# Dilated attention with the tokens of each block of 128 sorted by residue of 16, one stacked query tile and doubled key tiles

## The chip, the cores and the metric

The kernel runs on one core of a Trainium2 chip. The time is device microseconds (us) of one execution on that core; less is better. The engines are called as in the profile: PE (matrix products), PEld (its loading of the stationary operand), DVE (VectorE), ACT (ScalarE), POOL (GpSimd) and SP (it issues all DMAs here).

## What is computed

One decoder layer over 4096 tokens of width 1024, in float32. Eight attention heads of width 64 mix three dilated windows; four heads of width 128 run a gated linear recurrence (HGRN2). Both halves are normalised, gated, joined, projected, added to the input and normalised. The part that the change is about, cut from the reference:

```python
DILATED_PATTERNS = ((128, 1), (512, 4), (2048, 16))      # (window, dilation)

def _dilated_window_attn(q, k, v, window, dilation):
    # the sequence is split into `dilation` residue sub-sequences; on each a causal
    # band of width window//dilation = 128, swept in blocks of 128 queries
    qb, kb, vb = to_blocks(q), to_blocks(k), to_blocks(v)
    kw, vw = with_prev(kb), with_prev(vb)                 # the block before and this one
    scores = jnp.einsum('bhrnqe,bhrnke->bhrnqk', qb, kw) * (e ** -0.5)
    scores = jnp.where(mask, scores, -jnp.inf)
    m = jnp.max(scores, axis=-1)
    p = jnp.exp(scores - m[..., None])
    l = jnp.sum(p, axis=-1)
    o = jnp.einsum('bhrnqk,bhrnke->bhrnqe', p, vw)
    return from_blocks(o), from_blocks(m), from_blocks(l)
```

For each query the outputs `o` of the three dilations are weighted by `exp(m - max m)` and divided by the weighted sum of the `l`.

## The kernel before

Float32 products are made of two float32r parts, hi + lo. The work has three phases.

Phase 1 (to about 590 us) projects x for the first three pairs of attention heads, block of 128 tokens by block, and writes queries and keys transposed (feature on the partition, token along the row; hi and lo parts), values and gates to DRAM (`attn_rows`, L274).

Phase 2 (to about 2480 us) first projects the fourth pair of heads, then runs the four recurrence heads, two blocks at a time: `project_T` and `project_N` (L226, L240, their matmuls are L220), `hgrn_gates`, `hgrn_values`, `hgrn_block`. x for the next two blocks is loaded and split while this one runs: ACT writes `xhi` (L209), POOL writes `xlo = raw - xhi` (L210). In between, `take` (L614) advances a generator that emits attention work at a fixed rate, so that all eight heads are spread evenly; a scheduler then orders every engine's instructions by its own estimate of time. Each engine runs its list in order.

A head (L483) runs its patterns in the order d = 16, 4, 1. Each pattern has 16 calls of `score` (L413), two blocks of queries each. `score` makes, for each block, two products into one PSUM bank: the queries' 128 columns are the stationary operand, the keys' 128 or 256 columns stream as the moving operand. K1 holds the keys' hi part on partitions 0 to 63 and the lo part on 64 to 127; Q1 holds the queries' hi part twice, Q2 the lo part twice. For a dilation d the columns are taken with stride d from rows in token order:

```python
def cols(t, r, d, j, n, p=slice(None)):
    a = r + d * 128 * j
    return t[p, a : a + d * (128 * n - 1) + 1 : d]
```

So with d = 16 a block of queries is 128 floats that lie 64 bytes apart, with d = 4 they lie 16 bytes apart, with d = 1 side by side. Then DVE adds the mask and takes the row maximum (L434), ACT takes the exponential and the row sum (L436), `flip` (L440) transposes the weights on PE (L446) and splits them on ACT (L449) and DVE (L450), `weigh` (L453) multiplies them with the values, ACT copies one half (`other`, L461) and DVE adds it: for d = 16 and 4 into the tile OA at stride d (L528, L543), for d = 1 into o1 (L551). `exchange` (L467) sends the row maxima and sums of d = 16 and 4 through DRAM to bring them into token order; `arrive` (L477) fetches them into `nat`. After every eight blocks of d = 1, `finish` (L564) joins the patterns: DVE writes the three weighted outputs to `pr` (L589), POOL adds them into `num` (L592, L593), the norm factor `nrr` is worked out on DVE (its last step is L147), POOL multiplies (L600, L601), and SP issues the DMA of `num` to y_d (L602). The next head's queries and keys are loaded during d = 1 (L409 to L411).

Phase 3 is the output projection, the residual and the last norm.

Of the kernel before, what the change touches and what calls it, by code (L numbers as in the profile page):

```python
# [17 lines left out]
F32 = mybir.dt.float32  # L18
F32R = mybir.dt.float32r
# [8 lines left out]
S = 4096  # L28
# [21 lines left out]
def layer(ctx: ExitStack, tc: tile.TileContext, x, xT, xP, pos, w_in, w_out, nw, anw, hnw, lbraw, fnw,  # L50
# [21 lines left out]
    mask = const.tile([128, 256], F32, name="mask")  # L72
# [13 lines left out]
    nrstd = const.tile([128, NB], F32, name="nrstd")  # L86
# [35 lines left out]
    def lower_bounds():  # L122
        """1 - lower bound of the forget gates, to DRAM"""
# [12 lines left out]
    def rsqrt(pool, u, n, scale, eps, tag):  # L136
        """(u*scale + eps) ** -0.5, [128, n], with one Newton step"""
# [62 lines left out]
    def load_pair(t):  # L200
        """two blocks of x, transposed: four pairs of k tiles"""
# [12 lines left out]
    def accumulate(groups):  # L214
        """groups of products, each into its own columns of one bank"""
# [10 lines left out]
    def project_T(X, W):  # L226
        """the first 256 columns of the group, transposed, for two blocks"""
# [12 lines left out]
    def project_N(X, W):  # L240
        """the last 256 columns of the group, two blocks of rows"""
# [21 lines left out]
    def row_stats(b):  # L263
        r = rsqrt(p1p, ssq[:, b : b + 1], 1, 1.0 / D, EPS, "rs")
        V.tensor_copy(rstd[:, b : b + 1], r)
        V.tensor_scalar(nrstd[:, b : b + 1], r, -1.0, None, op0=ALU.mult)

    def sigm(e):
        """e = exp(-z) -> sigmoid(z), in place; the bound keeps Ln in its range"""
# [4 lines left out]
    def attn_rows(pool, p, b, ps, gv, pt_):  # L274
# [3 lines left out]
        # rotary on the first 16 dims of q and k  # L278
# [20 lines left out]
        # silu of the gate times the norm gain  # L299
# [50 lines left out]
    def hgrn_values(t, ps):  # L350
        """gates and values of two blocks, tokens on the partitions"""
# [5 lines left out]
        for n in range(2):  # L357
            b = 2 * t + n
            A.activation(gv[:, n], ps[:, 256 * n : 256 * (n + 1)], AF.Copy, scale=rstd[:, b : b + 1])
# [6 lines left out]
    def hgrn_block(hh, b, qd, kd, g):  # L366
# [46 lines left out]
    def score(h, d, r, j0, ml, loc):  # L413
        """exp(score - row maximum) of two blocks of queries, row maxima and sums"""
# [4 lines left out]
        for j in (j0, j0 + 1):  # L419
# [3 lines left out]
            T.matmul(o, cols(Q1, r, d, j, 1), cols(K1, *ks), start=True, stop=False)  # L423
            T.matmul(o, cols(Q2, r, d, j, 1), cols(K1, *ks), start=False, stop=True)  # L424
            parts.append((j, nk, o, off))
            off += 128 * nk
        for j, nk, o, off in parts:
# [6 lines left out]
            V.tensor_tensor_reduce(out=p_, in0=o, in1=mask[:, 256 - 128 * nk : 256], scale=-0.125, scalar=3e38,  # L434
# [5 lines left out]
    def flip(d, j0, nb, loc):  # L440
        """transpose the weights of two blocks of keys and split them"""
# [11 lines left out]
    def weigh(seq, out):  # L453
        """seq: (values, unit, first column block, blocks)"""
# [391 lines left out]
```

## Time and profile before

| | |
|---|---|
| Time, median of three runs (lowest, highest) | 2859.76 us (2859.27, 2865.69) |
| The profiled execution: span | 2859.0 us |
| Granted TensorE clock | 0.988 of full speed |
| DVE, ACT, POOL busy, share of the span | 67%, 62%, 32% |
| DMA moved | 387.64 MB, mean 136 GB/s |

Busy time of PE is modelled: matmuls are pipelined, and the duration of one is longer than the step from one to the next. What a matmul takes from PE is therefore read from the timeline, as the distance between its start and the start of the next one. In the windows a row gives, after the stretch and its length, the busy time of PE, PEld, DVE, ACT and POOL with the count of instructions in brackets, then the granted clock, the share of the DMA engines and GB/s. In the rows of instructions the last pair of numbers is the total busy time in us and the mean of one in ns.

The heads can be told apart by the 96 weight loads of L423 that each makes, 32 in each pattern. The fifth head's scores begin at 1563 us (d = 16), 1620 us (d = 4) and 1684 us (d = 1), its last score is at 1767 us, and the sixth head begins at 1791 us.

### The profile page before, as it was taken

To read this page: it belongs to the slowest core of one execution; us is meant where nothing else is said; L and a number is where in the kernel's file an instruction comes from. 1 tells how busy PE (TensorE), PEld (TensorE's weight loads), DVE (VectorE), ACT (ScalarE), POOL (GpSimd) and SP (SyncE) were. 2 spreads that over 40 slices of the span, in tenths; PEclk is the share of its full clock that TensorE was granted. 3 is DMA by queue.
4 is the path that set the end of the run, shared out by engine and by line. 5 is a ranking of instruction groups with operands and counts; after the bars stand their busy time and mean duration, and the time that the engine had idled before them with its cause. 6 is when DMAs were issued, how large, how long until landed. Compare 5 with 4: busy or idle time off the path is not lost.

```text
span 2859.0 us, 53619 instructions
## 1 busy us (share of the span) xinstructions
PE 2779.3 (97%) x17697; PEld 2505.0 (88%) x17697; DVE 1907.3 (67%) x5907; ACT 1761.3 (62%) x5174; POOL 913.8 (32%) x906
## 2 busy tenths in 40 slices
PE   7999999999999999999999999999999999999998
PEld 5888888878888999998999999999999999788887
DVE  6444444446787788788688688778878878844443
ACT  6444444447766777776777777777777777622222
POOL 2222222143344245235335335335434524300000
PEclk9999999999999999999999999999999999899999
DMA  6444444494475265255346355336436422643432
GB/s 217 141 140 140 144 140 137 139 247 144 138 211 144 78 161 130 78 152 147 90 124 158 82 150 151 100 93 164 115 97 173 124 78 71 185 147 133 137 136 85
DMA packets 448138, 387.64 MB, mean 136 GB/s; under 512 B 117064, under 2 KB 340724, under 8 KB 447860
## 3 DMA queue, kind: packets, MB, share of 16 engines
q1 hardware_dynamic: 447860, 384.21, 47.1%
q8 instruction: 141, 2.31, 0.4%
q14 instruction: 137, 1.12, 0.1%
HBM read 291.27 MB, written 92.82 MB: 134 GB/s over the span
## 4 chain that ended last, share of the span: by engine, by line
PE 54%; DVE 10%; ACT 3%; DMA 2%; issue 1%; POOL 0%; SPq 0%; ACTq 0%; POOLq 0%; DVEq 0%
PE proj L220 18%; PE att L423 5%; PE po L458 5%; PE att L424 4%; PE proj L196 4%; PE proj L195 4%; PE proj L197 4%; PE att L446 4%; PE hp L370 1%; DVE pt L434 1%; PE hp L742 1%; PE hp L372 1%; DVE pl L450 1%; PE hp L378 1%; PE hp L380 1%
## 5 line engine op out<-in xcount | busy, mean ns | idle before, releaser
L195 PE MATMUL proj<-whi,xhi 128*128 128x512 f32 x1280 | 510.8, 399 | 15.9 <-ACT whi L171 7.9
L197 PE MATMUL proj<-whi,xlo 128*128 128x512 f32 x1280 | 513.2, 401 | 0.0
L196 PE MATMUL proj<-wlo,xhi 128*128 128x512 f32 x1280 | 510.4, 399 | 1.3 <-DVE wlo L172 1.3
L210 POOL TENSOR_TENSOR xlo<-raw,xhi 128x512 fp32r<-128x512 f32 x256 | 336.5, 1319 | 385.1 <-ACT xhi L209 343.7
L434 DVE CUSTOM_DVE_ANT_0 pt<-att,mask 128x256 f32<-128x256 f32 (+1 forms) x768 | 271.7, 390 | 158.6 <-PE att L424 155.5
L220 PE MATMUL proj<-xhi,whi 128*128 128x256 f32 x1024 | 301.3, 294 | 6.4 <-DVE hz L329 2.4
L423 PE MATMUL att<-K,Q 128*128 128x256 f32 (+1 forms) x768 | 302.2, 401 | 2.5 <-DMA Q<-qk_d 1.3
L220 PE MATMUL proj<-xhi,wlo 128*128 128x256 f32 x1024 | 300.9, 294 | 0.9 <-DVE wlo L172 0.9
L195 PEld LDWEIGHTS proj<-whi,xhi 128*128 128x128 f32 x1280 | 242.6, 190 | 67.3 <-ACT whi L171 8.8
L220 PE MATMUL proj<-xlo,whi 128*128 128x256 f32 x1024 | 301.3, 294 | 0.0
L220 PE MATMUL proj<-whi,xhi 128*128 128x256 f32 x1024 | 298.0, 291 | 0.0
L220 PE MATMUL proj<-whi,xlo 128*128 128x256 f32 x1024 | 297.2, 290 | 0.0
L220 PE MATMUL proj<-wlo,xhi 128*128 128x256 f32 x1024 | 296.6, 290 | 0.0
L196 PEld LDWEIGHTS proj<-wlo,xhi 128*128 128x128 f32 x1280 | 242.1, 189 | 53.9 <-DVE wlo L172 3.2
L436 ACT ACTIVATE pt<-pt,ml 128x256 f32<-128x256 f32 (+1 forms) x512 | 238.3, 467 | 77.2 <-DVE ml L434 75.5
L197 PEld LDWEIGHTS proj<-whi,xlo 128*128 128x128 f32 x1280 | 242.3, 189 | 48.0
L424 PE MATMUL att<-K,Q 128*128 128x256 f32 (+1 forms) x768 | 276.6, 367 | 2.1 <-issue 2.1
L450 DVE TENSOR_TENSOR pl<-att,ph 128x512 fp32r<-128x512 f32 (+1 forms) x384 | 238.3, 624 | 45.6 <-ACT ph L449 42.0
L185 POOL TENSOR_TENSOR xlo<-raw,xhi 128x512 fp32r<-128x512 f32 x126 | 162.2, 1289 | 244.9 <-ACT xhi L184 220.6
L282 DVE SCALAR_TENSOR_TENSOR rot<-rt,rsin 128x32 f32<-128x32 f32 x128 | 56.1, 438 | 271.9 <-ACT rt L277 271.7
L449 ACT ACTIVATE ph<-att 128x512 fp32r<-128x512 f32 (+1 forms) x384 | 206.9, 542 | 49.7 <-PE att L446 45.1
L446 PE MATMUL att<-ident,pt 128*128 128x128 f32 x1368 | 223.5, 278 | 6.4 <-DVE nat L434 5.1
(201 smaller groups left out, 7388.5 us busy)
## 6 DMA issues: line engine op xcount, KB each, us to landing
raw<-xP SPq DMA_DIRECT2D x256, 256.0 KB, 3.6
raw<-xT SPq DMA_DIRECT2D x128, 256.0 KB, 2.8
qk_d<-stk SPq DMA_DIRECT2D x128, 256.0 KB, 2.9
vh<-v_d SPq DMA_DIRECT2D x128, 256.0 KB, 3.5
Q<-qk_d SPq DMA_DIRECT2D x224, 128.0 KB, 3.7
raw<-x SPq DMA_DIRECT2D x64, 256.0 KB, 2.6
v_d<-hl SPq DMA_DIRECT2D x128, 128.0 KB, 2.6
vh<-v_d SPq DMA_DIRECT2D x128, 128.0 KB, 2.5
```

Source lines behind the costliest of these rows:

```text
L195: T.matmul(ps, hi[:, c], whi, start=(k == 0), stop=False)
L196: T.matmul(ps, hi[:, c], wlo, start=False, stop=False)
L197: T.matmul(ps, lo[:, c], whi, start=False, stop=(k == KT - 1))
L210: G.tensor_tensor(lo, raw, hi.bitcast(F32), op=ALU.subtract)
L220: m = T.matmul(o, l, r, start=first is None, stop=(k == KT - 1 and g == len(groups) - 1 and n == 2))
L423: T.matmul(o, cols(Q1, r, d, j, 1), cols(K1, *ks), start=True, stop=False)
L424: T.matmul(o, cols(Q2, r, d, j, 1), cols(K1, *ks), start=False, stop=True)
L434: V.tensor_tensor_reduce(out=p_, in0=o, in1=mask[:, 256 - 128 * nk : 256], scale=-0.125, scalar=3e38, op0=ALU.add, op1=ALU.min, accum_out=m)
L436: A.activation(p_, p_, AF.Exp, scale=-1.0, bias=m, accum_out=l)
L446: T.transpose(ps[:, n * 128 : (n + 1) * 128], loc[u], ident)
L449: A.activation(ph[:, :w], ps[:, :w], AF.Copy)
L450: V.tensor_sub(pl[:, :w], ps[:, :w], ph[:, :w].bitcast(F32))
```

## The change

Within every block of 128 tokens the token `16 u + r` is stored in place `8 r + u`. A residue class of 16 is then a run of 8 neighbours in every block, 32 bytes, and a residue class of 4 is four such runs that lie 32 places apart. A band of a dilated pattern is read as runs of 8 floats.

What follows from it, edit by edit:

- The host gives x, its transpose for phase 1 and the positions in that order; the transpose for the recurrence stays in token order. The row norms of the recurrence are turned back (`rstdn`). The recurrence writes y with four DMAs for four blocks, rows in the new order, and `out` is written back in token order.
- The mask has one pair of triangles for each dilation, as the order within a block differs.
- Instead of K1, Q1, Q2 there are KH (hi twice), KL (lo twice) and QS (hi over lo). Both products of a block now have the same stationary queries. For d = 16 and 4 POOL first copies 512 query columns into a contiguous tile `qc` (two buffers), once for two calls of `score`: 16 copies a head, 128 in all. For d = 1 the queries are read in place.
- OA is written in runs of 8. The values are loaded with four DMAs instead of two (d = 16) or one (d = 4).
- `exchange` transposes the maxima and sums on PE, DVE copies them to `mt`, and four (d = 16) or eight (d = 4) DMAs write them, in place of two; `mt` and `mr` share one buffer.
- To make room, `num` lies in `pr` now, and `hrb` has one buffer instead of two.

The diff also empties comments, so that line numbers shift. Its core:

```diff
 def cols(t, r, d, j, n, p=slice(None)):
-    a = r + d * 128 * j
-    return t[p, a : a + d * (128 * n - 1) + 1 : d]
+
+    return t[p].rearrange("p (g r u) -> p r g u", r=d, u=8)[:, r, 16 * j : 16 * (j + n)]
...
-        rb = hp.tile([128, 256], F32, name="hrb", bufs=2)
+        rb = hp.tile([128, 256], F32, name="hrb", bufs=1)
...
-            dma(y_d[b0 * 128 : (b0 + 4) * 128, 512 + hh * 128 : 512 + (hh + 1) * 128].rearrange("(i p) c -> p i c", p=128),
-                gv[:, :, 128:256])
...
+            yv = y_d[b0 * 128 : (b0 + 4) * 128, 512 + hh * 128 : 512 + (hh + 1) * 128].rearrange("(i r u) c -> i u r c", r=16, u=8)
+            for i in range(4):
+                dma(yv[i], gv[:, i, 128:256])
...
-        for t, u0, u1 in ((K1, 1, 3), (Q1, 0, 0), (Q2, 2, 2)):
+        for t, u0, u1 in ((KH, 1, 1), (KL, 3, 3), (QS, 0, 2)):
             dma(t[0:64, cs].bitcast(F32), qk[:, u0, cs])
             dma(t[64:128, cs].bitcast(F32), qk[:, u1, cs])
...
+    def queries(d, r, j0):
+
+        if d == 1:
+            return QS[:, 128 * j0 : 128 * (j0 + 4)]
+        q = tp.tile([128, 512], F32R, name="qc", bufs=2)
+        if d == 16:
+            v = QS.rearrange("p (g r u) -> p r g u", r=16, u=8)[:, r : r + 2]
+            G.tensor_copy(q.rearrange("p (r g u) -> p r g u", r=2, u=8), v)
+        else:
+            G.tensor_copy(q.rearrange("p (g u) -> p g u", u=8), cols(QS, r, d, j0, 4))
+        return q
+
+    def score(h, d, r, j0, q, ml, loc):
...
-            T.matmul(o, cols(Q1, r, d, j, 1), cols(K1, *ks), start=True, stop=False)
-            T.matmul(o, cols(Q2, r, d, j, 1), cols(K1, *ks), start=False, stop=True)
+            T.matmul(o, q[:, j % 2 * 128 : (j % 2 + 1) * 128], cols(KH, *ks), start=True, stop=False)
+            T.matmul(o, q[:, j % 2 * 128 : (j % 2 + 1) * 128], cols(KL, *ks), start=False, stop=True)
...
+        ps = ps_t.tile([64, 128], F32, name="att")
+        T.transpose(ps, ml.rearrange("i q c -> i (q c)"), ident)
+        mt = tp.tile([64, 128], F32, name="mt", tag="mr", bufs=1)
+        V.tensor_copy(mt, ps)
         for q in range(2):
-            dma(md[q].rearrange("(b i r) -> i b r", i=128, r=d), ml[:, q, :].rearrange("i (b r) -> i b r", r=d))
...
+                for r in range(d):
+                    dma(mv[r], mt[32 * q + r : 32 * (q + 1) : d].rearrange("j (g u) -> j g u", u=8))
...
-                            for n2 in range(2):
-                                dma(vh[:, 2 * n2 : 2 * n2 + 2].bitcast(F32), sv[:, r + n2, :, i, :])
+                            for n2 in range(4):
+                                dma(vh[:, n2].bitcast(F32), sv[r + n2 // 2, n2 % 2, :, :, i, :])
...
-                        V.tensor_tensor(cols(OA, r, 4, j0, 4, slice(64, 128)), po[64:128], other(po, 64), op=ALU.add)
+                        V.tensor_tensor(cols(OA, r, 4, j0, 4, slice(64, 128)), po[64:128].rearrange("p (g u) -> p g u", u=8),
+                                        other(po, 64).rearrange("p (g u) -> p g u", u=8), op=ALU.add)
...
-        num = tp.tile([128, 8, 64], F32, name="num", bufs=1)
-        G.tensor_tensor(num, pr[:, :, 0], pr[:, :, 1], op=ALU.add)
+        num = pr[:, :, 1]
+        G.tensor_tensor(num, pr[:, :, 0], num, op=ALU.add)
...
-        "pos": np.ascontiguousarray(positions[0].reshape(NB, 128).T),
+        "pos": np.ascontiguousarray(positions[0].reshape(NB, 8, 16).transpose(2, 1, 0).reshape(128, NB)),
```

How the change moves instructions is seen at two places. The first is POOL's list at the fourth head's last `finish` and the start of the fifth head; numbers behind a name count its buffers. Before:

```order
L592 TENSOR_TENSOR num_19886<-pr_19692 128x512
L593 TENSOR_TENSOR num_19886<-num_19886,pr_19692 128x512
L363 TENSOR_TENSOR hgv_20173<-hgv_20173,heg_20513 128x2x128
L364 TENSOR_TENSOR hgv_20173<-hgv_20173,gv0H_16451 128x2x128
L600 TENSOR_TENSOR num_19886<-num_19886,nrr_19895 128x512
L601 TENSOR_TENSOR num_19886<-num_19886,sgt_19680 128x512
L210 TENSOR_TENSOR xlo_20884<-raw_20881,xhi_20883 128x512
L332 TENSOR_TENSOR hz_20799<-hz_20799,he_20800 128x256
L210 TENSOR_TENSOR xlo_20890<-raw_20887,xhi_20889 128x512
```

The same place after the change, where L622, L629 and L630 are the sums and products of `finish` and L420 is the copy of queries for d = 16:

```order
L622 TENSOR_TENSOR pr_20035<-pr_20035 128x8x64
L331 TENSOR_TENSOR hz_21546<-hz_21546,he_21547 128x256
L210 TENSOR_TENSOR xlo_21641<-raw_21638,xhi_21640 128x512
L420 COPY qc_20593<-QS_6195 128x512
L210 TENSOR_TENSOR xlo_21647<-raw_21644,xhi_21646 128x512
L344 TENSOR_TENSOR hqd_21564<-hz_21546,hea_21561 128x256
L420 COPY qc_20648<-QS_6195 128x512
L210 TENSOR_TENSOR xlo_22002<-raw_21999,xhi_22001 128x512
L362 TENSOR_TENSOR hgv_21250<-hgv_21250,heg_21619 128x2x128
L629 TENSOR_TENSOR pr_20035<-pr_20035,nrr_20237 128x8x64
L363 TENSOR_TENSOR hgv_21250<-hgv_21250,gv0H_16703 128x2x128
L630 TENSOR_TENSOR pr_20035<-pr_20035,sgt_20023 128x8x64
```

The copies stand between the `xlo` tiles of the recurrence's projection and the steps of `finish`, and wait for their turn behind these.

The second place is DVE's list between the norm factor of the fourth head's second `finish` (L147) and the first weighted output of the next `finish`. Before (L589 is that output):

```order
L147 TENSOR_TENSOR nrr<-nrr,nrq 128x8
L450 TENSOR_TENSOR pl<-att,ph 128x512
L329 TENSOR_TENSOR hz<-proj,hrb 128x512
L388 TENSOR_TENSOR hR<-hp_19949,hs 128x128
L270 TENSOR_SCALAR he<-he 128x512
L589 TENSOR_TENSOR pr<-att,wt 128x2x192 x2
```

After the change (L618 is that output):

```order
L147 TENSOR_TENSOR nrr<-nrr,nrq 128x8
L580 TENSOR_TENSOR o_19600<-po,pot 64x256
L462 TENSOR_TENSOR pl<-att,ph 128x512
L580 TENSOR_TENSOR o_19600<-po,pot 64x256
L334 SCALAR_TENSOR_TENSOR hcum<-keep,hcum 128x256
L336 TENSOR_SCALAR hhalf<-hcum 128x2
L339 TENSOR_SCALAR hcum<-hcum,hhalf 128x128 x2
L383 TENSOR_SCALAR hs<-hR,hea 128x128
L618 TENSOR_TENSOR pr<-att,wt 128x2x192 x2
```

The weighted outputs of the next `finish` have moved back by four instructions here. Counted over the three such places of each of the seven later heads, the distance from L147 to the first output is 7 instructions on the average before and 13 after.

More of the change, by code (lines that the diff above doesn't have):

```diff
@@ L433, in score @@
             p_ = pt[:, off : off + 128 * nk]
-            V.tensor_tensor_reduce(out=p_, in0=o, in1=mask[:, 256 - 128 * nk : 256], scale=-0.125, scalar=3e38,
+            V.tensor_tensor_reduce(out=p_, in0=o, in1=mask[:, (1, 4, 16).index(d), 256 - 128 * nk : 256], scale=-0.125, scalar=3e38,
                                    op0=ALU.add, op1=ALU.min, accum_out=m)
@@ L470, in exchange @@
         md = ml_d[h, di]
+        ps = ps_t.tile([64, 128], F32, name="att")
+        T.transpose(ps, ml.rearrange("i q c -> i (q c)"), ident)
+        mt = tp.tile([64, 128], F32, name="mt", tag="mr", bufs=1)
+        V.tensor_copy(mt, ps)
         for q in range(2):
-            dma(md[q].rearrange("(b i r) -> i b r", i=128, r=d), ml[:, q, :].rearrange("i (b r) -> i b r", r=d))
-        mr = tp.tile([32, 2, 128], F32, name="mr", bufs=1)
+            if d == 16:
+                mv = md[q].rearrange("(j g r u) -> j r g u", g=16, r=d, u=8)
+                for j in range(2):
+                    dma(mv[j], mt[32 * q + 16 * j : 32 * q + 16 * (j + 1)].rearrange("r (g u) -> r g u", u=8))
+            else:
+                mv = md[q].rearrange("(j g r u) -> r j g u", g=16, r=d, u=8)
+                for r in range(d):
+                    dma(mv[r], mt[32 * q + r : 32 * (q + 1) : d].rearrange("j (g u) -> j g u", u=8))
+        mr = tp.tile([32, 2, 128], F32, name="mr", tag="mr", bufs=1)
         dma(mr, md.rearrange("q (b i) -> b q i", i=128))
@@ L502, in head @@
                     _, r, j = ready[n]
-                    score(h, d, r, j, ml, loc[r])
+                    if n % 2 == 0:
+                        qc = queries(d, r, j)
+                    score(h, d, r, j, qc[:, 256 * (n % 2) : 256 * (n % 2 + 1)], ml, loc[r])
                     yield 1.0
@@ L511, in head @@
                         if d == 16:
-                            for n2 in range(2):
-                                dma(vh[:, 2 * n2 : 2 * n2 + 2].bitcast(F32), sv[:, r + n2, :, i, :])
+                            for n2 in range(4):
+                                dma(vh[:, n2].bitcast(F32), sv[r + n2 // 2, n2 % 2, :, :, i, :])
+                        elif d == 4:
+                            for n2 in range(4):
+                                dma(vh[:, n2].bitcast(F32), sv[r, j + n2, :, :, i, :])
                         else:
-                            dma(vh.bitcast(F32), sv[:, r, j : j + 4, i, :])
+                            dma(vh.bitcast(F32), v_d[p][j * 128 : (j + 4) * 128, i, :].rearrange("(j p) c -> p j c", p=128))
                         fl = {}
@@ L526, in head @@
                         po = weigh(seq, None)
-                        pv = po.rearrange("p (r u) -> p r u", r=2)
-                        V.tensor_tensor(OA[0:64].rearrange("p (u r) -> p r u", r=16)[:, r0 : r0 + 2, :],
-                                        pv[0:64], other(po, 0).rearrange("p (r u) -> p r u", r=2), op=ALU.add)
+                        pv = po.rearrange("p (r g u) -> p r g u", r=2, u=8)
+                        V.tensor_tensor(OA[0:64].rearrange("p (g r u) -> p r g u", r=16, u=8)[:, r0 : r0 + 2],
+                                        pv[0:64], other(po, 0).rearrange("p (r g u) -> p r g u", r=2, u=8), op=ALU.add)
                         yield 1.0
@@ L786, in final_norm @@
         V.scalar_tensor_tensor(xr, xr, r, fnwt, op0=ALU.mult, op1=ALU.mult)
-        dma(out[b * 128 : (b + 1) * 128, :], xr)
+        dma(out[b * 128 : (b + 1) * 128, :].rearrange("(u r) c -> r u c", r=16), xr)
     for b in range(2):
@@ L819 @@
     i = np.arange(128)
-    t1 = np.where(i[:, None] <= i[None, :], 0.0, NEG).astype(f)
-    t2 = np.where(i[:, None] >= i[None, :], 0.0, NEG).astype(f)
+    ms = []
+    for m in (16, 4, 1):
+        n = m * (i // (8 * m) * 8 + i % 8) + i // 8 % m
+        for lower in (False, True):
+            ms.append(np.where((n[:, None] >= n[None, :]) if lower else (n[:, None] <= n[None, :]), 0.0, NEG).astype(f))
     arrays = {
-        "x": xs,
+        "x": xc,
         "xT": xT,
         "xP": np.ascontiguousarray(xs.reshape(NB // 2, 256, KT, 128).transpose(0, 3, 2, 1)).reshape(NB // 2, 128, 2 * D),
-        "pos": np.ascontiguousarray(positions[0].reshape(NB, 128).T),
+        "pos": np.ascontiguousarray(positions[0].reshape(NB, 8, 16).transpose(2, 1, 0).reshape(128, NB)),
         "w_in": w,
```

31 lines of the change are left out of this document (16 added, 15 removed).

## The prediction

> **What bounds the kernel now.** I read the page's busy times first, then the windows of one head, then the timeline of PE inside them. The page:
>
> ```profile
> PE 2779.3 (97%) x17697; PEld 2505.0 (88%) x17697; DVE 1907.3 (67%) x5907; ACT 1761.3 (62%) x5174; POOL 913.8 (32%) x906
> ```
>
> PE looks full, but its durations overlap, so this alone proves nothing. The windows of the fifth head, in the order d = 16, d = 4, d = 1 and the last `finish` (columns as in the table's text: PE, PEld, DVE, ACT, POOL):
>
> ```profile
> 1563.00:1620.00 57.00, 57.00 (x419) 55.27 (x418) 42.78 (x142) 44.45 (x143) 25.29 (x24) 1.00 0.37 100
> 1620.00:1684.00 64.00, 63.94 (x458) 60.96 (x458) 45.88 (x137) 48.12 (x142) 16.03 (x16) 1.00 0.32 84
> 1684.00:1767.00 83.00, 81.29 (x669) 77.16 (x668) 72.98 (x215) 64.37 (x196) 40.00 (x37) 1.00 0.63 175
> 1767.00:1791.00 24.00, 20.97 (x175) 19.70 (x174) 22.36 (x49) 15.77 (x45) 15.36 (x16) 1.00 0.65 164
> ```
>
> In the first two PE has no idle time, while ACT is busy 78% and 75%. In d = 1 DVE is at 88% and PE idles 1.71 us (2%); in the last `finish` DVE is at 93% and PE idles 3.03 us (13%). So time taken off PE in d = 16 and d = 4 shortens the kernel until ACT or DVE comes near 90%.
>
> **What the strides cost PE.** The timeline of PE, one `score` call with d = 16, then two recurrence matmuls of 128 contiguous columns (first column start, second duration):
>
> ```profile
> 1572.12 0.36 PE L423 MATMUL att<-K,Q 128*128 128x128 f32 x1
> 1572.31 0.39 PE L424 MATMUL att<-K,Q 128*128 128x128 f32 x1
> 1572.52 0.50 PE L423 MATMUL att<-K,Q 128*128 128x256 f32 x1
> 1572.85 0.40 PE L424 MATMUL att<-K,Q 128*128 128x256 f32 x1
> 1573.06 0.30 PE L220 MATMUL proj<-xhi,wlo 128*128 128x256 f32 x1
> ...
> 1574.12 0.39 PE L378 MATMUL hp<-hgv,hk 128*128 128x128 f32 x2
> 1574.35 0.39 PE L380 MATMUL hp<-hgv,att 128*128 128x128 f32 x2
> ```
>
> Two calls with d = 4:
>
> ```profile
> 1641.23 0.58 PE L423 MATMUL att<-K,Q 128*128 128x256 f32 x1
> 1641.62 0.42 PE L424 MATMUL att<-K,Q 128*128 128x256 f32 x1
> 1641.86 0.42 PE L423 MATMUL att<-K,Q 128*128 128x256 f32 x1
> 1642.10 0.41 PE L424 MATMUL att<-K,Q 128*128 128x256 f32 x1
> 1642.34 0.30 PE L220 MATMUL proj<-whi,xlo 128*128 128x256 f32 x1
> ...
> 1642.60 0.49 PE L423 MATMUL att<-K,Q 128*128 128x256 f32 x1
> ...
> 1643.62 0.30 PE L220 MATMUL proj<-wlo,xhi 128*128 128x256 f32 x1
> ```
>
> One call with d = 1, where both operands are contiguous already:
>
> ```profile
> 1515.52 0.28 PE L423 MATMUL att<-K,Q 128*128 128x256 f32 x1
> 1515.64 0.29 PE L424 MATMUL att<-K,Q 128*128 128x256 f32 x1
> 1515.76 0.28 PE L423 MATMUL att<-K,Q 128*128 128x256 f32 x1
> 1515.88 0.28 PE L424 MATMUL att<-K,Q 128*128 128x256 f32 x1
> 1515.99 0.28 PE L220 MATMUL proj<-wlo,xhi 128*128 128x256 f32 x1
> ```
>
> The same four matmuls take 0.47 us with d = 1 and 1.11 and 1.02 us with d = 4, about 1.07. The call with d = 16 has two matmuls of 128 and two of 256 columns and takes 0.94 us; contiguous it would be 2 x 0.115 (L378: 0.23 for two) + 2 x 0.12 = 0.47.
>
> **The change part by part.**
>
> *PE's term.* If queries from `qc` and keys in runs of 8 go at the contiguous rate, d = 16 saves 16 x (0.94 - 0.47) = 7.5 us a head. d = 4 has, for each residue, one call like the one above (0.47 saved) and three of 256 columns throughout (1.07 - 0.48 = 0.59 saved): 4 x 0.47 + 12 x 0.59 = 9.0, together 16.5 a head. Eight heads: 132 us.
>
> Runs of 8 floats as a moving operand occur in no row. The upper end is the contiguous rate. The lower end is that keys stay as slow as now. That rate is seen alone where the weights loaded next are contiguous: from L424 to L220 it is 0.21 us (d = 16) and 0.24 us (d = 4) for 256 columns. Then d = 16 needs 2 x 0.115 + 2 x 0.21 = 0.65 and saves 0.29 x 16 = 4.6; d = 4 needs 0.96 in place of 1.07 (12 x 0.11 = 1.3) and 0.71 in place of 0.94 (4 x 0.23 = 0.9): 6.8 a head, 54 us. I take 132, since d = 4 steps 16 bytes and d = 16 64 bytes and both are slow by about the same factor: the price looks like one for every float that stands alone, not for distance.
>
> [...]
>
> *What becomes the next limit.* d = 16 shrinks from 57 to 49.5 us with ACT's 44.45 us unchanged (90%), d = 4 from 64 to 55 with 48.12 (87%). By the windows above PE then idles between 2% (companion at 88%) and 13% (93%); I take 3% of 104.5 us, 3.1 a head, 25 us in all. Ends: 0 and 13% (13.6 a head, 109 us).
>
> *DVE.* The writes to OA lose their stride:
>
> ```profile
> L543 DVE TENSOR_TENSOR OA<-po,pot 64x512 f32<-64x512 f32 x64 | 71.3, 1114 | 7.7 <-ACT pot L464 5.8
> L528 DVE TENSOR_TENSOR OA<-po,pot 64x512 f32<-64x512 f32 x64 | 66.8, 1044 | 5.8 <-ACT pot L464 5.8
> L450 DVE TENSOR_TENSOR pl<-att,ph 128x512 fp32r<-128x512 f32 x216 | 146.7, 683 | 22.5 <-ACT ph L449 20.3
> ```
>
> At L450's 0.68 they free 64 x 0.43 + 64 x 0.36 = 51 us of DVE (0 if runs of 8 do not help it). Against that stand POOL's 128 copies. Nearest rows: a one-input operation on 256 columns and a two-input one on 512.
>
> ```profile
> L113 POOL TENSOR_SCALAR kk<-kk 128x256 f32<-128x256 f32 x1 | 0.7, 722 | 0.1
> L592 POOL TENSOR_TENSOR num<-pr 128x512 f32<-128x512 f32 x32 | 42.7, 1334 | 44.9 <-DVE pr L589 30.0 <-PE proj L220 7.5 <-issue 6.4
> ```
>
> Between 0.72 and 1.33 I take 0.9, the nearer to the one-input row: 14.4 us a head on POOL's 96.7 (the four windows), so 111 of some 212. POOL is no bound, but DVE feels it. The duration of one DVE instruction on SBUF alone, min/median/max, and its mean:
>
> ```profile
> L340 DVE TENSOR_SCALAR hcum<-hcum,hhalf x128: 251/281/1385, 897.5 to 2457.9; 128x128 f32<-128x128 f32 x128
> ...
> L340 DVE TENSOR_SCALAR hcum<-hcum,hhalf 128x128 f32<-128x128 f32 x128 | 60.9, 512 | 1.4
> ```
>
> The mean is 0.23 us over the median, and the longest lasts about one POOL instruction more. POOL is busy 42% of the head; copies add 7 points, so about 0.04 us for each of some 150 such instructions in a head (counted in the code: about 13 for each two blocks, nine times, and nine in each `finish`): 6 us a head, 48 in all. It cancels the 51; I count 0, between -51 and +48. [...]
>
> *`num` inside `pr`.* The next `finish` may write `pr` only when the DMA of y has read it. The second `finish` of the fourth head, from DVE's and POOL's timelines and the DMA list:
>
> ```profile
> 1533.29 0.17 DVE L147 TENSOR_TENSOR nrr<-nrr,nrq 128x8 f32<-128x8 f32 x1
> 1536.15 1.01 DVE L589 TENSOR_TENSOR pr<-att,wt 128x384 f32<-128x384 f32 x2
> ...
> 1534.66 1.29 POOL L601 TENSOR_TENSOR num<-num,sgt 128x512 f32<-128x512 f32 x1
> ...
> y_d<-num SPq DMA_DIRECT2D x32, 256.0 KB, 3.5
> ```
>
> From L147 to the landing it takes 2.66 + 3.5 = 6.2 us; today L589 follows after 2.9. Behind a waiting L589 stand the score maxima and the recurrence's steps, which PE needs. The new order puts 13 instead of 7 instructions in between; at 0.40 us each (22.36/49 = 0.46 and 72.98/215 = 0.34 in the last two windows) that is 5.2 us, and 1.0 remains. Three such places a head: 24 x 1.0 = 24 us. Ends: 0 and 24 x 3.3 = 79.
>
> *Small terms.* Sixteen more transposes with their copies and the longer chain of `exchange`: PE has waited at `arrive` only this much in all,
>
> ```profile
> PE att L480 <- DVE nat L434: 0.6, 1, 0.6
> ```
>
> so there is slack; I put 0.4 us for each, 6 us. The new DMA issues (40 more a head for values, 8 for `exchange`, 96 for the recurrence's y) come on SP, which now waits long for its own turn:
>
> ```profile
> SPq L515 <- PE po L458: 125.1, 42, 13.1
> ```
>
> They fit into that slack, and cost nothing as long as it stays; without it, an issue delays only loads that are asked for early. `hrb` with one buffer is refilled when the last block pair's first DVE step is done, some 25 us ahead: nothing. Copies at a head's start behind POOL's `finish` steps: one POOL instruction, 0.75 us, eight times: 6 us. Phases 1 and 3 keep their work.
>
> *The sum*, on the span of 2859.0 us: -132 + 25 + 24 + 6 + 6 = -71, 2788. The median of the runs lies 0.8 us above the span: **2789 us**.
>
> **The rivals.**
>
> 1. *Everything hides* (chance 0.10): idle, `pr` and the small terms near 0. For it: PE is never idle now in d = 16 and 4. Against: ACT at 90%. 2859.8 - 132 = 2728, some 2735 with the transposes.
> 2. *The keys do not get faster* (0.10): the change then does half of what it says. 54 us gained, no new idle time as ACT stays at 85%, 36 us of other terms: 2842.
> 3. *ACT takes over* (0.08): 13% idle as in the last `finish`: -132 + 109 + 36 = +13, 2873; halfway it is no change.
> 4. *Copies queue on POOL* (0.10), the way to slower. POOL runs in order, and its `xlo` often wait:
>
> ```profile
> POOL xlo L210 <- ACT xhi L209: 343.7, 134, 16.1
> ```
>
> That is 2.6 us a time. A copy behind such a wait holds PE's two next calls of `score`. If half the 128 copies pass 2.6 us on, the price is 166 us: 2789 - 6 + 166 = 2949. It decides from 71/128 = 0.55 us a copy. Against it: two `qc` buffers give a copy the time of two calls, 57/8 = 7 us.
>
> **How the numbers follow.** The forecast holds 0.62. A measurement here tells 0.3% (8.6 us) from no change. Faster: 0.61 of the forecast, rivals 1 and 2, and 0.03 of rival 3, so 0.84; the same: 0.05; slower: 0.11. The range runs from rival 1 to rival 2, 2733 to 2842, and leaves out rivals 3 and 4.
>
> **What would show it.** The steps of the score matmuls with d = 16 and 4 at 0.12 us for 256 columns; at 0.21 rival 2 holds. The window of d = 16 near 51 us, of d = 4 near 57, with ACT near 88%. DVE waiting before L618 for the DMA of y, about 1 us a time. A copy near 0.9 us; PE waiting for `qc` would mean rival 4. If phases 1 or 3 change by over 3 us, I have missed a part.

## The result and the profile after

The changed kernel takes **2789.25 us** (median of 4 runs, 2788.09 to 2791.51), the kernel before in the same comparison 2859.52 us (4 runs, 2858.64 to 2865.69): ratio 0.9751, 95% interval 0.9737 to 0.9765. That is 70 us faster, and the forecast of 2789 us holds almost to the digit. Its terms hold less well, and that is what the rest is about.

The profiled execution has a span of 2788.2 us. Its page, the line of busy times:

```profile
PE 2672.7 (96%) x17714; PEld 2386.1 (86%) x17714; DVE 1875.9 (67%) x5892; ACT 1745.6 (63%) x5174; POOL 994.0 (36%) x1034
```

PE lost 106.6 us of busy time and the span 70.8: some 36 us came back as idle time. The timeline of PE, one `score` call with d = 16 and one with d = 4, each with the matmul behind it:

```profile
1572.22 0.23 PE L435 MATMUL att<-KH,qc 128*128 128x128 f32 x1
1572.28 0.27 PE L436 MATMUL att<-KL,qc 128*128 128x128 f32 x1
1572.39 0.35 PE L435 MATMUL att<-KH,qc 128*128 128x256 f32 x1
1572.57 0.31 PE L436 MATMUL att<-KL,qc 128*128 128x256 f32 x1
1572.72 0.29 PE L220 MATMUL proj<-xhi,whi 128*128 128x256 f32 x1
...
1635.87 0.28 PE L435 MATMUL att<-KH,qc 128*128 128x256 f32 x1
1635.98 0.28 PE L436 MATMUL att<-KL,qc 128*128 128x256 f32 x1
1636.10 0.28 PE L435 MATMUL att<-KH,qc 128*128 128x256 f32 x1
1636.22 0.28 PE L436 MATMUL att<-KL,qc 128*128 128x256 f32 x1
1636.34 0.28 PE L470 MATMUL po<-ph,vh 128*128 128x256 f32 x1
```

From the first start to the start of the next matmul it is 0.50 us (0.94 before) and 0.47 us (about 1.07 before). The d = 4 call runs at the rate of contiguous keys; d = 16 takes 0.03 us more than foreseen.

The windows of the fifth head, cut at the first score of each stage (PE, PEld, DVE, ACT, POOL, then clock, DMA share and GB/s):

```profile
1556.00:1609.00 53.00, 51.68 (x433) 49.86 (x431) 43.48 (x142) 44.62 (x146) 29.79 (x31) 1.00 0.39 104
1609.00:1662.00 53.00, 49.20 (x400) 46.67 (x400) 43.08 (x136) 46.81 (x140) 17.64 (x20) 1.00 0.44 126
1662.00:1750.00 88.00, 85.06 (x710) 80.47 (x710) 73.97 (x219) 65.21 (x201) 43.12 (x42) 1.00 0.62 157
1750.00:1775.00 25.00, 23.32 (x192) 22.01 (x192) 22.75 (x55) 16.11 (x48) 15.90 (x16) 1.00 0.54 144
```

d = 16 went from 57 to 53 us (foreseen 51) and d = 4 from 64 to 53 (foreseen 57), with ACT at 84% and 88%. PE, which had no idle time there, now idles 1.32 and 3.80 us. But d = 1 grew from 83 to 88 us, and its PE has 710 matmuls in place of 669: work that used to lie beside the slow scores now lies there. A stage by itself is therefore no measure of the gain. Summed over the seven later heads, from the starts of the first score of each stage (in us; a last `finish` is the stretch from one head's last score to the next head's first, and the seven of them begin with the first head's, so the columns do not add up to the last one):

| | d = 16 | d = 4 | d = 1 | last `finish` | second head's first score to the last score |
|---|---|---|---|---|---|
| before | 416 | 447 | 570 | 167 | 1574 |
| after | 375 | 382 | 592 | 183 | 1508 |

The two strided stages gave 106 us, the other two took 38 back. Ahead of the second head and behind the last score only 5 us of the 71 were won.

The whole attention phase in one window, before and then after, in which PE's idle time is the length less its busy time:

```profile
590.00:2481.00 1891.00, 1835.79 (x13403) 1736.43 (x13402) 1481.66 (x4368) 1375.52 (x4128) 767.46 (x725) 0.99 0.49 131
```

```profile
590.00:2410.20 1820.20, 1729.73 (x13426) 1618.64 (x13424) 1450.36 (x4377) 1360.70 (x4127) 847.61 (x853) 0.98 0.51 138
```

PE work fell by 106.1 us, PE idle time rose from 55.2 to 90.5. Everything in the result is these two numbers: -106 + 35 = -71. The phases ahead of it and behind it changed by some 3 us: PE starts its 2,500th matmul at 578 us before and 581 after, and from the 16,000th of the 17,714 to the end it takes 372 us before and 369 after (before counted in the same proportion).

The groups of DVE and POOL that the prediction priced (busy time, mean ns | idle before):

```profile
L571 DVE TENSOR_TENSOR OA<-po,pot 64x512 f32<-64x512 f32 x64 | 44.5, 695 | 6.6 <-ACT pot L476 4.9
L556 DVE TENSOR_TENSOR OA<-po,pot 64x512 f32<-64x512 f32 x64 | 43.3, 677 | 5.7 <-ACT pot L476 5.6
L339 DVE TENSOR_SCALAR hcum<-hcum,hhalf 128x128 f32<-128x128 f32 x128 | 67.1, 562 | 1.4
L420 POOL CAST qc<-QS 128x512 fp32r<-128x512 f32 x64 | 40.7, 643 | 48.0 <-PE att L436 41.8 <-DMA QS<-qk_d 5.6 <-DMA raw<-xP 0.6
L422 POOL CAST qc<-QS 128x512 fp32r<-128x512 f32 x64 | 39.6, 618 | 112.1 <-PE att L436 111.7 <-PE proj L220 0.3
```

The writes to OA take 0.68 and 0.70 us in place of 1.04 and 1.11, as forecast. A copy takes 0.63 us, less than the 0.9 assumed. The copies wait for PE (L436 gives their buffer back), so they run ahead of it; no wait of a matmul names `qc`, and one weight load waited for it, for 0.4 us. The DVE instruction in which the prediction saw the collisions with POOL went from a mean of 512 to 562 ns, +0.05 us (foreseen +0.04); the kernel without copies shows below that the copies are not the reason.

Last, the place at which `pr` is held. In the third `finish` of the fourth head POOL ends the last product (L630) at 1545.5 us. The timeline of SP's queue, which then issues the DMA of y (L631):

```profile
1538.38 0.53 SPq L206 DMA_DIRECT2D raw<-xP  x1
1545.68 0.64 SPq L403 DMA_DIRECT2D y_d<-hgv  x1
...
1550.20 0.54 SPq L631 DMA_DIRECT2D y_d<-pr  x1
```

and the timeline of DVE, where the next `finish` begins with L618:

```profile
1550.38 0.35 DVE L383 TENSOR_SCALAR hs<-hR,hea 128x128 f32<-128x128 f32 x1
1554.90 1.49 DVE L618 TENSOR_TENSOR pr<-att,wt 128x384 f32<-128x384 f32 x3 [4.18 <-DMA y_d<-pr]
```

DVE stands 4.18 us. The DMA itself was issued 4.7 us after its data were ready, because SP had waited from 1538.9 to 1545.7 for the recurrence's y (L403, which the change splits into smaller DMAs) and then had seven issues ahead of it. This is the longest of the seven waits of this kind. Among the 24 places where another `finish` follows in the same head, the y DMA was issued that late here alone; elsewhere it was under 2 us. In the kernel before, one of the 24 left late as well, by 5.5 us. DVE's list of waits (us in all, times, longest) has two entries that it did not have before:

```profile
DVE pr L618 <- DMA y_d<-pr: 10.4, 7, 4.2
DVE hz L328 <- DMA hrb<-rstd_d: 9.4, 4, 3.1
```

The second is the load of `hrb`, which has one buffer now.

### The profile page after: what moved, and what is told of

It reads as the page before. It is cut to its first block, busy times and chain, and to the rows that moved or that the text cites. A ratio compares the mean times of both kernels' runs of the same rounds, so it can differ in the third digit from the quotient of the medians.

```text
span 2788.2 us, 54611 instructions
## 1 busy us (share of the span) xinstructions
PE 2672.7 (96%) x17714; PEld 2386.1 (86%) x17714; DVE 1875.9 (67%) x5892; ACT 1745.6 (63%) x5174; POOL 994.0 (36%) x1034
## 5 line engine op out<-in xcount | busy, mean ns | idle before, releaser
L220 PE MATMUL proj<-xhi,whi 128*128 128x256 f32 x1024 | 298.6, 292 | 11.3 <-ACT whi L171 9.8
L220 PE MATMUL proj<-xlo,whi 128*128 128x256 f32 x1024 | 300.0, 293 | 0.3 <-POOL xlo L210 0.3
L220 PE MATMUL proj<-xhi,wlo 128*128 128x256 f32 x1024 | 299.7, 293 | 0.1
L220 PE MATMUL proj<-wlo,xhi 128*128 128x256 f32 x1024 | 298.0, 291 | 0.0
L220 PE MATMUL proj<-whi,xhi 128*128 128x256 f32 x1024 | 297.9, 291 | 0.0
L220 PE MATMUL proj<-whi,xlo 128*128 128x256 f32 x1024 | 297.1, 290 | 0.0
L470 PE MATMUL po<-ph,vh 128*128 128x128 f32 (+1 forms) x856 | 216.6, 278 | 5.9 <-ACT ph L461 3.1
L470 PE MATMUL po<-pl,vh 128*128 128x128 f32 (+1 forms) x856 | 210.9, 289 | 3.7 <-DVE pl L462 3.5
```

The lines of the kernel that those rows point to most:

```text
L220: m = T.matmul(o, l, r, start=first is None, stop=(k == KT - 1 and g == len(groups) - 1 and n == 2))
L470: T.matmul(po[:, 128 * c : 128 * (c + n)], v, rh, start=(s == 0), stop=(s == len(steps) - 1))
```

## The experiments

The theory after the result: PE's work falls by what the steps say, and idle time comes back from three places, the `pr` hold (24 us), the copies (6 us by the forecast) and DVE or ACT near their limit (25 us). The rivals: the copies cost much more than 6, or the hold costs nothing, or one engine alone is the new bound. The kernel before measured 2859.5 to 2862.9 us (medians) in the different comparisons, so differences between kernels of different comparisons are good to some 3 us. In every phase window below, idle is the length less PE's busy time, as above (90.5 us in the changed kernel).

### Are runs of 8 and the copies what made the matmuls fast?

Keys put back to their stride, with queries copied as now; then queries at their stride, with keys in runs (`cold` takes columns at distance d):

```diff
-            T.matmul(o, q[:, j % 2 * 128 : (j % 2 + 1) * 128], cols(KH, *ks), start=True, stop=False)
+            T.matmul(o, q[:, j % 2 * 128 : (j % 2 + 1) * 128], cold(KH, *ks), start=True, stop=False)
```

```diff
-            T.matmul(o, q[:, j % 2 * 128 : (j % 2 + 1) * 128], cols(KH, *ks), start=True, stop=False)
+            T.matmul(o, cold(QS, r, d, j, 1), cols(KH, *ks), start=True, stop=False)
```

The line with KL changes in the same way, and the second kernel makes no copies.

> The changed kernel with the keys alone read at the old stride of d floats (the rows are in the new order, so these are other keys); queries still come from the contiguous copies. Theory of the forecast: PE loses 6.9 us in d = 16 and d = 4 of each head's 16.5, so 78 us more PE work, of which the idle time gives 10 to 25 back: 2842 to 2865; 256 columns step at 0.21 to 0.24 us. Rival (slow loading of the stationary operand was the whole price, and the strided stream hides behind it): 2790 to 2810.

> The changed kernel with the queries alone read at the old stride of d floats, without copies (other queries); keys in runs of 8. Theory of the forecast: each weight load takes 0.21 us or more again, so a call of four matmuls needs 0.85 in place of 0.47, 0.38 x 32 calls x 8 heads = 97 us more, of which 10 to 25 come back: 2860 to 2880. Rival (the price of before came from both operands being strided at once): 2800 to 2830.

Measured: 2844.9 us (ratio 0.9941, 0.9927 to 0.9954) with keys strided, 2872.5 us (1.0038, 1.0024 to 1.0051) with queries strided. Their attention phases, keys first:

```profile
590.00:2465.10 1875.10, 1793.98 (x13416) 1670.74 (x13415) 1447.16 (x4371) 1367.31 (x4125) 845.28 (x851) 0.98 0.48 133
```

```profile
590.00:2492.30 1902.30, 1827.45 (x13423) 1725.42 (x13422) 1427.59 (x4374) 1375.25 (x4127) 767.12 (x723) 0.98 0.47 132
```

PE's work rises by 64 and 98 us, and PE's idle time falls by 9 and 16. The strides are the cause, of both operands, and the queries (loaded as weights) weigh more. The median step from the first to the second matmul of 256 columns, in d = 16 and in d = 4, was 0.32 and 0.31 us before; it is 0.22 and 0.23 with keys strided, 0.29 and 0.23 with queries strided, and 0.18 and 0.12 now. Both results lie inside what the theory gave. The two prices do not add up: 64 and 98 us are together more than the 106 of the whole change. With the queries strided PE's work is within 9 us of the kernel before, so keys in runs gain almost nothing as long as the queries stay strided. The kernel with keys strided also lies 3 us from the 2842 of the prediction's rival 2 (keys that do not get faster), but this is luck: the rival had 54 us of PE's work gained and 36 us lost elsewhere, while against the kernel before this one saves 42 us of PE's work, of which 26 us come back as idle time.

### Does the distance between runs matter?

Keys of d = 16 are runs of 8 floats 512 bytes apart, those of d = 4 are 128 bytes apart. This kernel exchanges the distances:

```diff
-            ks = (r, d, j - nk + 1, nk)
+            ks = (r, d, j - nk + 1, nk) if d == 1 else (r % 4, 4, j - nk + 1, nk) if d == 16 else (r, 16, 0, nk)
```

> The changed kernel with the distances between the runs of keys exchanged: d = 16 reads runs of 8 that lie 128 bytes apart, d = 4 runs that lie 512 bytes apart (other keys in both). The profile of the changed kernel has 256 columns at 0.18 and 0.15 us in d = 16 and at 0.12 in d = 4. Theory of the forecast (the length of the run alone counts): nothing moves with the distance, d = 16 stays slow for another reason, 2789 plus or minus 5. Rival (distance counts): d = 16 steps at 0.12 and d = 4, with 28 such pairs a head against 16, at 0.15 to 0.18: 10 to 20 us more.

Measured: 2784.1 us (0.9727, 0.9714 to 0.974). The timeline of PE, d = 16 (now 128 bytes apart) and then d = 4 (now 512 bytes):

```profile
1571.52 0.22 PE L435 MATMUL att<-KH,qc 128*128 128x128 f32 x1
1571.58 0.28 PE L436 MATMUL att<-KL,qc 128*128 128x128 f32 x1
1571.69 0.33 PE L435 MATMUL att<-KH,qc 128*128 128x256 f32 x1
1571.86 0.29 PE L436 MATMUL att<-KL,qc 128*128 128x256 f32 x1
1571.98 0.29 PE L220 MATMUL proj<-xhi,whi 128*128 128x256 f32 x1
...
1642.97 0.30 PE L435 MATMUL att<-KH,qc 128*128 128x256 f32 x1
1643.10 0.30 PE L436 MATMUL att<-KL,qc 128*128 128x256 f32 x1
1643.24 0.32 PE L435 MATMUL att<-KH,qc 128*128 128x256 f32 x1
1643.38 0.31 PE L436 MATMUL att<-KL,qc 128*128 128x256 f32 x1
1643.53 0.29 PE L220 MATMUL proj<-whi,xhi 128*128 128x256 f32 x1
```

d = 16 falls from 0.50 to 0.46 us a call, d = 4 rises from 0.47 to 0.56: with 512 bytes between runs, 256 columns take 0.14 us in place of 0.12. So distance does count, by some 0.02 us per matmul. The step of 0.17 from the third matmul stays at either distance: the pair of 128 columns ahead of it starts 0.06 apart, and the 256 columns seem to pay that back, as the whole call (0.06 + 0.11 + 0.17 + 0.12 = 0.46 us) comes to the 0.47 of contiguous operands. By these calls the exchange adds 0.09 x 12 us a head with d = 4 and takes 0.04 x 16 with d = 16, some 4 us more in eight heads; the kernel came out 5 to 8 us faster. A change this small in PE's steps does not show in the total, and the time by itself, at the edge of the theory's 2789 plus or minus 5, would have hidden that the theory was wrong on the distance.

### What is the hold of `pr` worth?

The last product of `finish` goes into the tile of the gate, and the DMA of y reads that, so `pr` is free as soon as POOL has read it:

```diff
-        G.tensor_tensor(num, num, sg, op=ALU.mult)
-        dma(y_d[bs, 64 * h : 64 * h + 64].rearrange("(i p) c -> p i c", p=128), num)
+        G.tensor_tensor(sg, num, sg, op=ALU.mult)
+        dma(y_d[bs, 64 * h : 64 * h + 64].rearrange("(i p) c -> p i c", p=128), sg)
```

> The changed kernel with the last product of finish written into the tile of the gates, from which the DMA of y then reads: pr is free when POOL has read it and not when the DMA has. Theory of the forecast (the wait for the DMA costs 24 us, and most of what was given back lies in d = 1 and finish): 2765 to 2775, and DVE no longer waits for the DMA of y. Rival (the scheduler has filled that wait with other work, and the loss sits elsewhere): 2785 to 2792.

Measured: 2765.8 us (0.9666, 0.9652 to 0.9679). Its attention phase:

```profile
590.00:2385.10 1795.10, 1720.13 (x13420) 1614.84 (x13419) 1451.12 (x4372) 1365.11 (x4126) 845.90 (x851) 0.98 0.51 139
```

The wait for the DMA of y is gone from DVE's list, PE idles 75.0 us in place of 90.5, and PE's own durations fall by 9.6. By the same sums as in the table above, d = 1 and the last `finish` give back 30 us, and the strided stages take 12 more. It is 23 us faster than the change, near the 24 that the prediction had set for the hold. The waits in the trace were 10.4 us, so the gain is more than their length; that the steps behind a waiting DVE start later too is a likely reason, but it was not isolated. It beats both the kernel before and the change, by 3.3% and 0.8%.

The same hold by itself in the kernel before:

```diff
-        num = tp.tile([128, 8, 64], F32, name="num", bufs=1)
-        G.tensor_tensor(num, pr[:, :, 0], pr[:, :, 1], op=ALU.add)
+        num = pr[:, :, 1]
+        G.tensor_tensor(num, pr[:, :, 0], num, op=ALU.add)
```

> The kernel before with num inside pr and nothing else. Theory of the forecast (a wait of up to 3.3 us at 24 places, of which the new order takes away all but 1.0 us): 2859 goes to 2875 to 2890. Rival (the order fills the wait): 2857 to 2864.

Measured: 2869.1 us (1.0022, 1.0012 to 1.0032), 6 us slower. DVE's wait and the attention phase:

```profile
DVE pr L589 <- DMA y_d<-pr: 7.6, 4, 3.2
590.00:2488.30 1898.30, 1833.34 (x13397) 1732.88 (x13395) 1481.60 (x4350) 1372.48 (x4119) 767.23 (x723) 0.99 0.48 130
```

DVE waits 7.6 us for the DMA of y, not much less than in the change, and PE idles 65.0 us in place of 55.2; yet the hold costs a quarter of what it costs in the change. The result lies between the theory and the rival, and the theory fell: the hold has no fixed price. What makes the difference of 17 us is open. The scores with d = 16 and 4 are faster in the change, but the `finish` steps lie in d = 1, where the scores step at 0.12 us in both kernels, and the two also differ in the copies, the DMA issues and the order.

### What do the copies cost?

Contiguous queries without copies, by taking any 512 columns of QS in place:

```diff
-        q = tp.tile([128, 512], F32R, name="qc", bufs=2)
...
-        return q
+        k = r // 2 if d == 16 else 2 * r + j0 // 4
+        return QS[:, 512 * k : 512 * (k + 1)]
```

> The changed kernel without POOL's 128 copies: for d = 16 and 4 the stationary queries are read in place from contiguous columns that are not the right ones, so the scores are of other queries. Theory of the forecast (PE sets the pace, POOL has room): the copies cost only the small terms, so 2789 goes to 2780, at most 10 us less. [...]

Measured: 2768.3 us (0.9674, 0.9661 to 0.9687), 21 us faster than the change. Its attention phase:

```profile
590.00:2389.40 1799.40, 1725.88 (x13427) 1617.10 (x13426) 1446.88 (x4380) 1362.17 (x4128) 767.48 (x724) 0.98 0.50 139
```

PE idles 73.5 us, 17 less. The 21 us are twice the 10 that the theory allowed. PE starts its 7,000th matmul 6 us earlier than in the change, its 7,500th 15 us earlier and its 14,500th 20 us earlier: nearly half of the 21 comes in one stretch, the end of the third head, and the rest is spread. DVE's wait for the DMA of y, and the DVE instruction in which the prediction saw the collisions with POOL:

```profile
DVE pr L613 <- DMA y_d<-pr: 13.7, 7, 3.3
L339 DVE TENSOR_SCALAR hcum<-hcum,hhalf 128x128 f32<-128x128 f32 x128 | 72.8, 605 | 1.8
```

The wait is longer than in the change (10.4 us) in a kernel that is 21 us faster, so its length does not tell its price. And the mean of L339 is 605 ns without any copy, against 562 with them: its rise from 512 does not need the copies. DVE's busy time falls by only 3.5 us, so DVE instructions that take longer beside the copies can hold but a small part of the 21.

To tell the copies' work from the waiting for them, this kernel makes the copies but reads the queries in place:

```diff
-        return q
+        k = r // 2 if d == 16 else 2 * r + j0 // 4
+        return QS[:, 512 * k : 512 * (k + 1)]
```

> The changed kernel with POOL's 128 copies made and never read: PE reads contiguous queries in place (other queries), so no copy waits for PE and PE waits for none. Theory that the 21 us of the copies are the coupling of POOL's list to PE (153 us of POOL waiting for a free qc): 2765 to 2772, as without copies. [...]

Measured: 2823.9 us (0.9864, 0.9851 to 0.9878), 35 us slower than the change. The theory had 17 to 24 us less than the change and misses by over 50. What else is new here is the order: with no reader, the copies need not wait, and the scheduler has put them elsewhere on POOL. POOL's timeline around the last `finish` of the fourth head, in this kernel:

```profile
1550.64 1.17 POOL L420 CAST qc<-QS 128x512 fp32r<-128x512 f32 x2 [2.22 <-DMA QS<-qk_d]
1551.76 0.72 POOL L362 TENSOR_TENSOR hgv<-hgv,heg 128x256 f32<-128x256 f32 x1
1552.43 1.16 POOL L420 CAST qc<-QS 128x512 fp32r<-128x512 f32 x2
...
1557.70 1.05 POOL L630 TENSOR_TENSOR pr<-pr,nrr 128x512 f32<-128x512 f32 x1 [3.40 <-DVE nrr L147]
1558.69 0.61 POOL L420 CAST qc<-QS 128x512 fp32r<-128x512 f32 x1
...
1562.12 1.70 POOL L631 TENSOR_TENSOR pr<-pr,sgt 128x512 f32<-128x512 f32 x1
```

Four copies stand ahead of the two last steps of `finish` (L630 and L631), the first of them waiting for the load of the next head's queries with POOL's other work behind it, and a fifth stands between the two. The stretch from a head's last score to the next head's first is 27 to 41 us, where the change has 23 to 33. Its attention phase:

```profile
590.00:2444.40 1854.40, 1743.83 (x13422) 1626.83 (x13421) 1445.92 (x4377) 1360.95 (x4128) 838.44 (x852) 0.98 0.49 135
```

PE idles 20 us more than in the change, and its durations grow by 14, with nearly the same busy time on DVE, ACT and POOL. So the same 80 us of copies cost 21 us in the change and 56 here (against the kernel without them), by where they stand and who waits; that they stood in the way of `finish` is the likely reason, but it was not isolated. How the 21 us divide between the copies' work and the waiting for them stays open.

### Is one engine the new bound?

Row sums left out of the exponentials, which takes 57 us off ACT's busy time in the phase (POOL writes ones as the sums); then the low part of the weights left out, which takes 172 us off DVE's:

```diff
-            A.activation(p_, p_, AF.Exp, scale=-1.0, bias=m, accum_out=l)
+            A.activation(p_, p_, AF.Exp, scale=-1.0, bias=m)
```

```diff
-        V.tensor_sub(pl[:, :w], ps[:, :w], ph[:, :w].bitcast(F32))
-        return {u: (ph, pl, n * 128) for n, u in enumerate(units)}
+        return {u: (ph, ph, n * 128) for n, u in enumerate(units)}
```

> The changed kernel without the row sums of the exponentials (768 reads of the accumulator at 0.19 us, 146 us of ACT; the denominators are ones). Theory of the forecast (ACT near 90% leaves PE idle 3% in d = 16 and 4): 2760 to 2775. Rival (ACT is the limit now): 2700 to 2750. Rival (DVE, not ACT, is what PE waits for): 2782 to 2790.

> The changed kernel without the low parts of the weights on DVE (384 subtractions, 239 us of DVE); PE multiplies the high parts twice in their place, so its work is the same. Theory of the forecast (DVE at 88 to 93% in d = 1 and finish leaves PE idle there): 2745 to 2770, with the gain in d = 1 and finish. Rival (DVE has room, PE's own work is all that is left): 2780 to 2790.

Measured: 2768.6 us (0.9679, 0.9664 to 0.9693) and 2753.9 us (0.962, 0.9606 to 0.9634). Their attention phases:

```profile
590.00:2388.30 1798.30, 1721.92 (x13418) 1613.96 (x13416) 1446.38 (x4370) 1303.79 (x3355) 849.09 (x871) 0.98 0.50 138
```

```profile
590.00:2372.00 1782.00, 1707.94 (x13432) 1607.59 (x13431) 1278.54 (x4009) 1360.90 (x4131) 848.91 (x855) 0.99 0.51 140
```

-21 us for 57 us of ACT (0.36 for each) and -35 us for 172 us of DVE (0.2 for each). The expectations had counted the sums of the instructions' own durations, 146 and 239 us, and the busy times fell by less; by those sums it is 0.14 and 0.15 for each. The gain without the low parts is not in d = 1 and `finish` alone, where the expectation had it: 21 us lie there and 15 in the strided stages. Neither engine is the bound by itself, and with either of them relieved PE still idles 74 to 76 us. Removing the hold, the copies, some ACT work or some DVE work each ends at nearly the same idle time (73.5 to 76.4), above the 55.2 of the kernel before. No single one of the four reaches that; two of them together were not run.

### Is it only the order of instructions?

Each of these edits lets the scheduler write a new order on every engine, so the order itself had to be tested. Two kernels that only load QS, KL and KH in other orders (the first also the values), and the kernel without the hold in the first of these orders:

```diff
-        for t, u0, u1 in ((KH, 1, 1), (KL, 3, 3), (QS, 0, 2)):
+        for t, u0, u1 in ((QS, 0, 2), (KL, 3, 3), (KH, 1, 1)):
```

```diff
-        for t, u0, u1 in ((KH, 1, 1), (KL, 3, 3), (QS, 0, 2)):
+        for t, u0, u1 in ((KL, 3, 3), (QS, 0, 2), (KH, 1, 1)):
```

> A control: the changed kernel with the same work, where the DMAs of a head's queries and keys, and the four of its values, are issued in the reverse order; the scheduler then writes out another order on every engine. If differences of 20 us between variants are read rightly as the price of what was taken out, this one stays at 2789 plus or minus 5. Rival (the order that the scheduler happens to find is worth as much): 10 us or more away, to either side.

> A second control: the changed kernel with the DMAs of a head's lo keys first, then the queries, then the hi keys. If the order is worth little: 2789 plus or minus 5. Rival (the order is worth 10 us or more): anywhere from 2765 to 2800.

> The kernel with pr free before the DMA, under the other order of loads of the control. If the gain of 23 us belongs to pr, it lies 18 to 28 us under the control and near 2766. If it belongs to the order, the two lie within 10 us.

Measured: 2791.6 us (0.9751, 0.9738 to 0.9764) and 2790.5 us (0.9751, 0.9735 to 0.9768) for the orders, 2771.0 us (0.9679, 0.9666 to 0.9692) without the hold. Two other orders move the time by some 2 us, and the hold is worth 21 us in the other order too, so its 23 us are not chance of the order. For the 21 us of the copies the two controls say the same, but less firmly: the copies were not taken out under another order, and the kernel with copies unread shows that an order can cost 35 us.

## Why the prediction came out right

*PE's term* (forecast -132). The distances from the start of a score matmul to the next start, summed over all of them with the waits in between, fell from 333 to 206 us: -126, 61 of it in d = 16 (forecast 60), 66 in d = 4 (forecast 72) and +1 in d = 1. The mechanism was right, and the two strided kernels show it. The choice of 132 over 54 rested on the price being for each float that stands alone, not for distance; that holds for runs 128 bytes apart (0.12 us for 256 columns) and is 0.02 us per matmul off at 512 bytes (0.14). Without the waits the steps fell by 122 us, but PE's busy time in the phase fell by 106: the other matmuls of the window take 16 us more, spread over nearly every group. Some 4 of these are 30 more projection matmuls inside the window, as phase 1 ends some 3 us later; the rest is open.

*What becomes the next limit* (forecast 25), *the hold* (24), *small terms* (6 and 6): 61 in all, against 35 us of new idle time. The hold is confirmed at 21 to 23, but not by its working: that had 1.0 us at each of 24 places, and the trace has seven waits, 10.4 us in all. That the size came out is luck. The copies cost 21 where the forecast had 6, and this is the step that failed: "Copies at a head's start behind POOL's `finish` steps: one POOL instruction, 0.75 us, eight times" looked at one delay a head and not at 128 instructions put between others on an engine that runs in order. No run prices the 25 for ACT and DVE near their limits: relief of ACT or DVE brought 21 and 35 us, which is what that work is worth and not what the change cost. Taken alone, the hold and the copies gave back 15.5 and 17.0 us of idle time, together nearly the whole 35. If the two add, little is left for the 25; no run takes out both.

So the total was right to the digit since two errors cancelled, which is luck: by the busy time PE's work fell by 26 us less than forecast and idle time rose by 26 us less. By the scores' steps the two errors are smaller, 6 us each: 126 in place of 132, and 55 of it given back in place of 61.

*DVE's term* (forecast 51 freed, 48 taken). OA's writes freed 50 (71.3 + 66.8 before, 44.5 + 43.3 now). The collisions took far less than 48: DVE's busy time fell by 31 us in the phase, which leaves 19 for them and all else. The working had gone wrong twice. Its 7 points of POOL's load are 10 by its own figures (96.7 of 228 us, then 111 of 212), which would have given some 66 us. And the instruction it was read from rose by 0.05 us, as if foreseen, but the copies are not needed for that: without them its mean is higher still (605 ns). At 0.2 us for each us of DVE this is worth some 6 us, so counting it as nothing was a small error in the end.

*SP's new issues* (forecast nothing) were nearly that: at one place of 24 the DMA of y left 4.7 us late, behind the recurrence's y, and one place of the kernel before is as late. *`hrb`* with one buffer (forecast nothing) did cost waits, 9.4 us of DVE; with the first of the other load orders they are 0.9 us and the time is no shorter, so nothing shows that they cost time. *`exchange`* (forecast 6) stayed within it. PE's wait for its result, in the list of PE's waits (at this place it waited 0.6 us in all before):

```profile
PE att L503 <- DMA mr<-ml_d: 3.7, 4, 2.4
```

*The rivals.* The first (everything hides, 2735) did not come, since PE idles 35 us more; the change without hold and copies would be near it at 2745 if the two gains added, which was not run. The second is excluded by the steps. Of the third (ACT takes over, 13% idle) there is 5% (90.5 of 1820.2 us), and relief of ACT alone brings 21 us. The fourth, copies that queue on POOL, had the right engine in a weak form: 21 us in place of 166, as two buffers let the copies run ahead and no PE wait names them; the kernel with copies unread shows that a worse place on POOL is not far away.

## What to carry to other kernels

Take the strides of both matmul operands off PE by laying the data out once in short runs (here a call of four score matmuls went from 0.94 and about 1.07 us to 0.50 and 0.47), and price it by the steps between starts, not by busy time. When that shortens the work of the engine that was full, a wait elsewhere can get dearer: try each one on the new kernel (here a reused buffer, 6 us in the old kernel and 23 in the new), and write the output from a tile that nobody needs next. What small new instructions cost on an engine that runs its list in order can differ with where they stand (here 80 us of copies cost 21 us in one order and 56 in another), so look at their place too.

## What the runs showed of the hardware

Runs of 8 floats as moving operand go at 0.12 us per 256 columns when 128 bytes apart (the d = 4 call of the changed kernel) and 0.14 when 512 bytes apart (the d = 4 call with the distances exchanged), against 0.21 and 0.24 for single floats 64 and 16 bytes apart (the kernel before, from L424 to L220). Weights at a stride take longer too: in the kernel before the mean weight load was 307 to 311 ns with d = 16 and 323 to 332 ns with d = 4 (the first and the second of a pair), and in the changed kernel it is 190 to 192 ns with the queries copied contiguous. A POOL copy of 512 columns with runs of 8 on the reading side takes 0.62 to 0.64 us in the changed kernel and 0.61 at the median with the copies unread, about half of a two-input POOL instruction of that size (1.33 us, L592 before). The DVE instruction L339 (128 x 128, operands in SBUF) takes 0.28 us, at most 0.29, the 70 times of 128 that no POOL instruction overlaps it, and 0.90 us on the average the 58 times that one does (in the kernel before, L340: 0.28 us 84 times and 0.96 us 44 times); without the copies the mean of all 128 is 0.605 us, against 0.562 with them.
